# Stick-breaking heads: softplus of the last two key blocks added on the vector engine; blocks 0 and 1 multiply that sum instead of each block

## The chip, the cores and the metric

The kernel runs on one core of a Trainium2 chip. The metric is the time of one execution on the device in microseconds (us), as a median over runs; a profiled execution has its own time, which is given beside it. The core's engines are TensorE (PE in the profile, with its weight loads as PEld), VectorE (DVE), ScalarE (ACT), GpSimd (POOL) and SyncE (SP), which here only issues DMAs. Each engine takes its instructions in the order in which they were written into its own stream.

## The reference, cut to what matters

One transformer block over 512 tokens and 1024 channels: an adaptive modulation, sixteen stick-breaking attention heads of width 64, four retention heads, gates, a projection, and a feed-forward part. The change is in the stick-breaking heads, whose computation is this:

```python
def stick_breaking_attention(q, k, v):
    ...
    for i in range(s_len // BLOCK):
        end = (i + 1) * BLOCK
        ...
        z = jnp.einsum('bhtd,bhsd->bhts', qb, kb).astype(jnp.float32) * scale
        mask = s_pos[None, :] < t_pos[:, None]
        log_1m_beta = jnp.where(mask, jax.nn.log_sigmoid(-z), 0.0)
        after = lax.cumsum(log_1m_beta, axis=3, reverse=True) - log_1m_beta
        log_a = jax.nn.log_sigmoid(z) + after
        a = jnp.where(mask, jnp.exp(log_a), 0.0)
        outs.append(jnp.einsum('bhts,bhsd->bhtd', a.astype(v.dtype), vb))
```

For each query, log_sigmoid(-z) (which is minus the softplus of z) is summed over all later keys. A key block of 128 keys needs the sum inside the block and the full sums of every later block.

## The kernel before

**Tiling.** Activations lie with channels or keys on the 128 partitions and the 512 tokens along the row. Every product is made with operands split into a high and a low part (`split`, L205: ScalarE rounds a copy to the high part in L207, VectorE subtracts it for the low part in L209 or L210), so that one full product is three matmuls, and a product whose left side is exact (the triangle of minus ones `negtri`, the matrix of minus ones `negones`) is two. All matmuls are issued in the helper at L229.

**One head** (`sb_head`, L594). The scores stand with keys on the partitions and queries along the row. Key block j only meets queries from 128*j on, so the blocks are 512, 384, 256 and 256 columns wide. `GEO` (L111) gives each block its bank of the head's three `z` banks: block 0 is bank 0, block 1 is bank 1, and blocks 2 and 3 share bank 2, block 2 in columns 0 to 255 and block 3 in columns 256 to 511. The head then runs:
1. eight score matmuls, two for each block (L599), out of the tiles `q`;
2. softplus, bank by bank in the order 2, 1, 0: mask (VectorE, L607), minus the magnitude (VectorE, L609), Exp and Ln (ScalarE, L612 and L613), add the positive part (VectorE, L614), and a split into a tile `s` (L616);
3. the suffix sums, added on TensorE into the same `z` bank: for each block `negtri` times its own softplus and `negones` times that of every later block (L622 to L627), two matmuls for each term; then Exp (L630) and another split, which gives the attention weights of that bank;
4. eight matmuls with the values into one bank `av` (L639), a copy of it on ScalarE (L642), a DMA that moves half of it to the other partitions (L644, `t<-t`), and an add on VectorE (L645) that gives the head's output in `o`.

**What feeds a head.** `sb_qk` (L574) makes the queries and keys of a pair of heads: two products of 24 matmuls each into two `ps` banks, a split into two `qp` tiles (L561, L562), and eight DMAs (L567 to L570) that copy these into three `q` tiles, one for the keys of both heads and one for the queries of each.

**What runs between.** While a head waits for VectorE and ScalarE, TensorE works on products that depend on no head: `sb_qk` of later pairs and the branch gates (`mix`, 24 matmuls each into one `ps` bank). This text calls them filler. The loop at L1098 runs four groups of two pairs (four heads): it makes pairs 2g+2 and 2g+3 and some gates behind the heads of group g. Heads are numbered 0 to 15 and pairs 0 to 7 here. After the heads come the projections of `acts` (L1113 to L1131), which read all head outputs.

**What sets the order.** A scheduler sets the order on each engine in this part of the program when the kernel is built, by its own estimates of time and by free buffers; on the chip each engine then follows that order and waits at semaphores. The buffers that matter are in `BUFS` (L94): `q=8` tiles, `qp=2`, `ps=4` banks, `z=3` banks (one head's), `av=1`, `s=8`. A buffer is written again only when all readers of the tile before it are done. All loads go through the one queue of SP, in the order of its stream; a load that waits holds those behind it.

Of the kernel before, what the change touches and what calls it, by code (L numbers as in the profile page):

```python
# [19 lines left out]
P = 128  # L20
# [90 lines left out]
GEO = ((0, 0, 0, 512), (1, 0, 128, 384), (2, 0, 256, 256), (2, 256, 256, 256))  # L111
# [4 lines left out]
def kernel(  # L116
# [9 lines left out]
    nc = tc.nc  # L126
# [22 lines left out]
    def pair(tag):  # L149
        return apool.tile([P, 2, S], F32R, tag=tag, bufs=BUFS[tag], name=nm(tag))  # L150
# [44 lines left out]
    negtri = cpool.tile([P, P], F32R, name="negtri")  # L195
# [32 lines left out]
    def mm(o, lhs, rhs, start, stop):  # L228
        return nc.tensor.matmul(o, lhs, rhs, start=start, stop=stop, skip_group_check=True).ins  # L229
# [208 lines left out]
    with tc.manual_schedule(engines={nc.vector.engine, nc.scalar.engine, nc.tensor.engine}):  # L438

        nc.scalar.preload_act_table_set("natural_log_exp_and_others")  # L440
        c = sm[:, SM_C : SM_C + KT]
# [152 lines left out]
    def sb_head(h):  # L594
        q, k, vt = sbq[h], sbk[h], sbv[h // 4]
        z = [psz(), psz(), psz()]
        for j in (3, 2, 1, 0):
            bank, c, t0, w = GEO[j]
            for i in range(2):  # L599
                head_pe[h] = mm(z[bank][:, c : c + w], k[:, j * P : (j + 1) * P], q[:, i, t0:S],  # L600
                                i == 0 and j != 2, i == 1)
        sp = {}
        for bank in (2, 1, 0):
            w = BANKW[bank]
            zb = z[bank][:, :w]
            m = S if bank == 2 else P
            nc.vector.tensor_tensor(zb[:, :m], zb[:, :m], maskc[:, :m], op=ALU.min)  # L607
            t = tmp()[:, :w]
            nc.vector.tensor_scalar(  # L609
                t.bitcast(I32), zb.bitcast(I32), -(2**31), None, op0=ALU.bitwise_or  # L610
            )
            nc.scalar.activation(t, t, AF.Exp)  # L612
            nc.scalar.activation(t, t, AF.Ln, bias=1.0)  # L613
            nc.vector.scalar_tensor_tensor(t, zb, 0.0, t, op0=ALU.max, op1=ALU.add)  # L614
            hl = pair("s")
            split(hl[:, 0, :w], hl[:, 1, :w], t)  # L616
            sp[bank] = hl
        avs = {}
        for bank in (2, 1, 0):
            for j in (3, 2) if bank == 2 else (bank,):  # L620
                _, c, t0, w = GEO[j]
                terms = [(negtri, j, t0)] + [(negones, jj, GEO[jj][2]) for jj in range(j + 1, 4)]  # L622
                for lhs, jj, tt in terms:
                    bj, cj, tj, wj = GEO[jj]
                    for i in range(2):
                        mm(z[bank][:, c + tt - t0 : c + w], lhs, sp[bj][:, i, cj : cj + wj],
                           False, False)  # L627
            w = BANKW[bank]
            t = tmp()[:, :w]
            nc.scalar.activation(t, z[bank][:, :w], AF.Exp)  # L630
            hl = pair("s")
            split(hl[:, 0, :w], hl[:, 1, :w], t)
            avs[bank] = hl
        o = psa()
        r, hf = (h % 4) // 2, h % 2
        for j in (3, 2, 1, 0):
            bank, c, t0, w = GEO[j]
            v = vt[j // 2][:, j % 2, r * 256 + hf * P : r * 256 + hf * P + P]
            for i in range(2):  # L639
                mm(o[:, t0:S], v, avs[bank][:, i, c : c + w], j == 3 and i == 0, j == 0 and i == 1)  # L640
        u, u2 = tmp(), tmp()
        nc.scalar.activation(u, o, AF.Copy)  # L642
        own, oth = (slice(0, HD), slice(HD, P)) if hf == 0 else (slice(HD, P), slice(0, HD))
        nc.sync.dma_start(u2[own], u[oth])  # L644
        nc.vector.tensor_add(o_sb[h // 2][own], u[own], u2[own])  # L645
# [1082 lines left out]
```

## Time and profile before

| what | value |
|---|---|
| median of 3 runs | 1173.23 us (1172.66 to 1174.77) |
| profiled execution, its span | 1173.1 us |
| instructions on PE | 6476 matmuls, 1156.8 us busy (99% of the span) |
| DVE, ACT busy | 873.2 us (74%), 611.9 us (52%) |
| DMA | 192.88 MB, 164 GB/s mean |

The span runs from the first to the last instruction of the core. A group's row gives the number of instructions, the time in which any of them ran, and the mean length of one; matmuls are pipelined, so that the length of one (its latency) is longer than the distance at which the next one starts. In a timeline row the columns are start, length of the merged stretch, engine, line, operation, tiles, shapes and count. The heads lie between about 490 and 728 us.

### The profile page before, as it was taken

The page shows a single profiled execution, that of the slowest core. Times are in us where ns is not written, and L with a number is a line of the kernel's source. Part 1 is how long each engine was busy: PE and PEld are TensorE (multiplying, and loading weights), DVE is VectorE, ACT ScalarE, POOL GpSimd, SP SyncE. Part 2 cuts the span into 40 slices and gives each one's busy share as a digit, 9 for nine tenths or more (in the row PEclk, how much of TensorE's full clock was granted, in tenths as well). Part 3 has the DMA queues.
Part 4 walks back from the last instruction along what each step waited for, and adds up shares of the span by engine and source line. Part 5 has one row for each costly group of instructions (what it writes and reads, how often), then busy time and mean ns, then how long its engine had stood idle before and what let it go on. Part 6 is the DMA issues. An engine that isn't in the chain of part 4 may idle for free.

```text
span 1173.1 us, 16899 instructions
## 1 busy us (share of the span) xinstructions
PE 1156.8 (99%) x6476; PEld 1010.9 (86%) x6476; DVE 873.2 (74%) x1342; ACT 611.9 (52%) x928; POOL 50.1 (4%) x84
## 2 busy tenths in 40 slices
PE   8999999999999999999999999999999999999996
PEld 7898888888878888888888888879999999999996
DVE  7979966775764867478888688775998776777556
ACT  5444543343333444478778688354954444454433
POOL 0000000020002010000000000000100000000000
PEclk9999999999999999999999999999999999999999
DMA  9723536493566565846565545873545663565232
GB/s 358 256 68 113 185 103 208 154 260 115 161 201 176 181 159 185 232 123 180 153 173 133 153 126 179 283 235 103 113 136 179 184 161 116 148 186 152 86 89 72
DMA packets 64017, 192.88 MB, mean 164 GB/s; under 512 B 7744, under 2 KB 9920, under 8 KB 63936
## 3 DMA queue, kind: packets, MB, share of 16 engines
q1 hardware_dynamic: 56624, 172.92, 46.3%
q0 software_dynamic: 6768, 18.35, 8.8%
q8 instruction: 51, 0.84, 0.3%
q10 hardware_dynamic: 544, 0.52, 0.1%
q14 instruction: 30, 0.25, 0.1%
HBM read 146.15 MB, written 18.87 MB: 141 GB/s over the span
## 4 chain that ended last, share of the span: by engine, by line
PE 89%; DVE 4%; DMA 3%; ACT 2%; issue 1%; SPq 0%; DVEq 0%; ACTq 0%
PE ps L229 65%; PE z L229 21%; PE av L229 3%; DMA raw<-wp 2%; DMA araw<-wada 1%; DVE sraw L387 1%; ACT whi L207 1%; DVE wlo L209 1%; DMA o<-xT 0%; ACT s L207 0%; DVE wlo L418 0%; DVE t L425 0%; DVE araw L257 0%; DMA gspill<-g 0%; DVE t L476 0%
## 5 line engine op out<-in xcount | busy, mean ns | idle before, releaser
L229 PE MATMUL ps<-h,whi 128*128 128x512 f32 (+1 forms) x1410 | 416.9, 377 | 1.6 <-DVE h L209 0.8
L229 PEld LDWEIGHTS ps<-h,whi 128*128 128x128 f32 x1410 | 256.2, 188 | 47.7 <-ACT h L431 1.8
L229 PE MATMUL ps<-h,wlo 128*128 128x512 f32 (+1 forms) x705 | 262.1, 376 | 0.0
L207 ACT ACTIVATE whi<-raw 128x1024 fp32r<-128x1024 f32 (+1 forms) x122 | 127.4, 1044 | 192.3 <-PE ps L229 144.8
L209 DVE TENSOR_TENSOR wlo<-raw,whi 128x1024 fp32r<-128x1024 f32 (+1 forms) x122 | 146.6, 1204 | 61.9 <-ACT whi L207 60.8
L229 PEld LDWEIGHTS ps<-h,wlo 128*128 128x128 f32 x705 | 132.8, 188 | 23.2
L229 PE MATMUL ps<-s,whi 128*128 128x512 f32 x480 | 148.5, 390 | 0.7 <-DVE v L209 0.6
L229 PE MATMUL z<-q,whi 128*128 128x256 f32 x504 | 106.8, 283 | 0.0
L229 PEld LDWEIGHTS ps<-s,whi 128*128 128x128 f32 x480 | 89.2, 188 | 19.3 <-DVE v L209 1.0
L229 PE MATMUL ps<-s,wlo 128*128 128x512 f32 x240 | 93.4, 389 | 0.0
L207 ACT ACTIVATE s<-t 128x512 fp32r<-128x512 f32 (+1 forms) x134 | 74.4, 586 | 34.8 <-DVE t L789 21.4
L209 DVE TENSOR_TENSOR s<-t,s 128x512 fp32r<-128x512 f32 (+1 forms) x134 | 81.3, 637 | 9.6 <-ACT s L207 9.3
L229 PEld LDWEIGHTS z<-q,whi 128*128 128x128 f32 x504 | 84.9, 192 | 1.5
L1166 DVE SCALAR_TENSOR_TENSOR o<-ps,mod,o 128x512 f32<-128x512 f32 (+1 forms) x63 | 42.4, 680 | 32.6 <-PE ps L229 32.6
L229 PEld LDWEIGHTS ps<-s,wlo 128*128 128x128 f32 x240 | 45.1, 188 | 9.5
L877 ACT ACTIVATE whi<-s 128x1024 fp32r<-128x1024 f32 x33 | 34.9, 1056 | 33.6 <-PE ps L229 19.0
L229 PE MATMUL ps<-whi,h 128*128 128x512 f32 (+1 forms) x192 | 52.4, 354 | 0.0
L881 DVE TENSOR_TENSOR wlo<-s,whi 128x1024 fp32r<-128x1024 f32 x32 | 39.1, 1222 | 16.3 <-ACT whi L877 15.9
L229 PE MATMUL ps<-q,whi 128*128 128x256 f32 (+1 forms) x224 | 49.3, 313 | 0.0
L229 PE MATMUL z<-qp,whi 128*128 128x256 f32 x168 | 47.2, 283 | 0.0
L229 PE MATMUL z<-q,wlo 128*128 128x256 f32 x168 | 46.4, 283 | 0.0
L257 DVE SCALAR_TENSOR_TENSOR araw<-araw,cact 128x1024 f32<-128x1024 f32 x32 | 38.4, 1221 | 10.0 <-DMA araw<-wada 9.8
(311 smaller groups left out, 2063.1 us busy)
## 6 DMA issues: line engine op xcount, KB each, us to landing
raw<-wp SPq DMA_DIRECT2D x151, 512.0 KB, 4.0
araw<-wada SPq DMA_DIRECT2D x32, 512.0 KB, 4.5
araw<-wp SPq DMA_DIRECT2D x26, 512.0 KB, 4.6
sraw<-wada SPq DMA_DIRECT2D x16, 512.0 KB, 7.8
q<-qp SPq DMA_DIRECT2D x32, 256.0 KB, 3.7
s<-wp SPq DMA_DIRECT2D x12, 512.0 KB, 5.2
spill<-o POOLq DMA_DIRECT2D x24, 256.0 KB, 7.2
o<-xT SPq DMA_DIRECT2D x16, 256.0 KB, 3.7
```

The source lines that it names most:

```text
L207: nc.scalar.activation(dst_hi, src, AF.Copy, scale=scale)
L209: return (eng or nc.vector).tensor_sub(dst_lo, src, f(dst_hi))
L229: return nc.tensor.matmul(o, lhs, rhs, start=start, stop=stop, skip_group_check=True).ins
L257: nc.vector.scalar_tensor_tensor(raw, raw, 1.0, cact, op0=ALU.mult, op1=ALU.mult, accum_out=col)
L387: nc.vector.scalar_tensor_tensor(raw, raw, 1.0, cact, op0=ALU.mult, op1=ALU.mult, accum_out=col)
L877: nc.scalar.activation(hi, t, AF.Copy)
L881: nc.vector.tensor_sub(lo, t, f(hi))
L1166: return nc.vector.scalar_tensor_tensor(x1[d][:, hv], o[:, hv], mod[:, gcol + d : gcol + d + 1], x1[d][:, hv], op0=ALU.mult, op1=ALU.add,)
```

## The change

For each head, VectorE adds the softplus of block 3 to that of block 2 (256 columns, in place in the tile `t`), and the sum is split into a new tile `late` out of the `q` buffers. Blocks 1 and 0, which needed `negones` times block 2 and `negones` times block 3, now take `negones` times `late`. Block 2 still takes block 3 by itself, and block 0 still takes block 1. The suffix sums go from 20 matmuls a head to 16; the four that are gone are 256 columns wide.

```diff
--- before.py
+++ after.py
@@ -615,16 +615,24 @@
             hl = pair("s")
             split(hl[:, 0, :w], hl[:, 1, :w], t)
             sp[bank] = hl
+            if bank == 2:
+                late = pair("q")
+                nc.vector.tensor_add(t[:, 0:256], t[:, 0:256], t[:, 256:512])
+                split(late[:, 0, 0:256], late[:, 1, 0:256], t[:, 0:256])
         avs = {}
         for bank in (2, 1, 0):
             for j in (3, 2) if bank == 2 else (bank,):
                 _, c, t0, w = GEO[j]
-                terms = [(negtri, j, t0)] + [(negones, jj, GEO[jj][2]) for jj in range(j + 1, 4)]
-                for lhs, jj, tt in terms:
-                    bj, cj, tj, wj = GEO[jj]
+                terms = [(negtri, t0, sp[bank][:, :, c : c + w])]
+                if j == 2:
+                    terms.append((negones, 256, sp[2][:, :, 256:512]))
+                elif j < 2:
+                    if j == 0:
+                        terms.append((negones, P, sp[1][:, :, 0:384]))
+                    terms.append((negones, 256, late[:, :, 0:256]))
+                for lhs, tt, x in terms:
                     for i in range(2):
-                        mm(z[bank][:, c + tt - t0 : c + w], lhs, sp[bj][:, i, cj : cj + wj],
-                           False, False)
+                        mm(z[bank][:, c + tt - t0 : c + w], lhs, x[:, i, :], False, False)
             w = BANKW[bank]
             t = tmp()[:, :w]
             nc.scalar.activation(t, z[bank][:, :w], AF.Exp)
```

The scheduler works out a new order for everything from the first head on. In what follows names carry the number that the build gave them, and lines behind the diff are 8 higher in the changed kernel.

**SP's queue, the loads of the queries and keys of pair 4 (heads 8 and 9).** `q_1007` and `q_1015` are the keys, `q_1008`, `q_1009`, `q_1016` and `q_1017` the queries of the two heads; `t<-t` is the half of a head's output that changes partitions, `t_941` of head 4, `t_1004` of head 7. Before:

```order
L567 DMA q_1008_5266<-qp_1005_5259 64x1024
L568 DMA q_1008_5266<-qp_1005_5259 64x1024
L644 DMA t_941_4931<-t_940_4930 64x512
L202 DMA raw_1114_5819<-wp 128x1024
L569 DMA q_1007_5265<-qp_1006_5260 64x512
L567 DMA q_1009_5271<-qp_1005_5259 64x1024
L570 DMA q_1007_5265<-qp_1006_5260 64x512
L568 DMA q_1009_5271<-qp_1005_5259 64x1024
L569 DMA q_1007_5265<-qp_1006_5260 64x512
L570 DMA q_1007_5265<-qp_1006_5260 64x512
```

With the change:

```order
L202 DMA raw_1158_6024<-wp 128x1024
L567 DMA q_1016_5266<-qp_1013_5259 64x1024
L568 DMA q_1016_5266<-qp_1013_5259 64x1024
L569 DMA q_1015_5265<-qp_1014_5260 64x512
L570 DMA q_1015_5265<-qp_1014_5260 64x512
L567 DMA q_1017_5271<-qp_1013_5259 64x1024
L652 DMA t_1004_5193<-t_1003_5192 64x512
L568 DMA q_1017_5271<-qp_1013_5259 64x1024
L569 DMA q_1015_5265<-qp_1014_5260 64x512
L570 DMA q_1015_5265<-qp_1014_5260 64x512
```

The eight loads stood around the output copy of head 4; they now stand behind six more weight loads, and the last three of them behind the output copy of head 7.

**TensorE, the scores of head 8 and the first suffix sum of its bank 2.** `z_1038`, `z_1037`, `z_1036` before and `z_1046`, `z_1045`, `z_1044` now are banks 2, 1 and 0 of head 8; `ps` rows are filler; `av_994` and `av_1002` are head 7's. Before (the rows left out are filler):

```order
L229 MATMUL z_1037_5439<-q_1008_5266,q_1007_5265 128x384 x2
L229 MATMUL z_1036_5438<-q_1008_5266,q_1007_5265 128x512 x2
L229 MATMUL ps_1109_5787<-h_57_256,whi_1112_5791 128x512
L229 MATMUL ps_1109_5787<-h_57_256,wlo_1113_5792 128x512
L229 MATMUL av_994_5183<-s_993_5180,v_745_3838 128x512
L229 MATMUL ps_1109_5787<-h_68_303,whi_1112_5791 128x512 x2
...
L229 MATMUL ps_1110_5788<-h_57_256,whi_1115_5821 128x512 x2
L229 MATMUL z_1038_5440<-s_1040_5455,negtri_96 128x256
```

With the change:

```order
L229 MATMUL ps_1122_5788<-h_118_532,whi_1127_5821 128x512
L229 MATMUL ps_1122_5788<-h_118_532,wlo_1128_5822 128x512
L229 MATMUL av_1002_5183<-s_1001_5180,v_745_3838 128x512
L229 MATMUL z_1046_5440<-q_1016_5266,q_1015_5265 128x256 x4
L229 MATMUL z_1045_5439<-q_1016_5266,q_1015_5265 128x384 x2
L229 MATMUL z_1044_5438<-q_1016_5266,q_1015_5265 128x512 x2
L229 MATMUL ps_1134_5866<-h_40_217,whi_1136_5869 128x512
L229 MATMUL z_1046_5440<-s_1048_5455,negtri_96 128x256
L229 MATMUL ps_1134_5866<-h_40_217,whi_1136_5869 128x512
L229 MATMUL z_1046_5440<-s_1048_5455,negtri_96 128x256 x3
```

Before, 25 matmuls of filler and two of `av` stand between the last scores of head 8 and its first `negtri`; now one matmul of filler stands there, and its bank `ps_1134` is the one that `ps_1023`, the queries of pair 5, has held.

**TensorE, the suffix sums of head 15, the last one.** `z_1215`, `z_1214`, `z_1213` before and `z_1230`, `z_1229`, `z_1228` now are its banks 2, 1 and 0; `q_1233` is its `late`; `ps_1256` and `ps_1272` are the last gate. Before:

```order
L229 MATMUL ps_1256_6636<-h_90_398,wlo_1259_6640 128x512
L229 MATMUL z_1215_6366<-s_1217_6381,negtri_96 128x256
L229 MATMUL ps_1256_6636<-h_101_445,whi_1258_6639 128x512 x2
L229 MATMUL z_1214_6365<-s_1219_6390,negtri_96 128x384
L229 MATMUL z_1215_6366<-s_1217_6381,negtri_96 128x256 x3
L229 MATMUL z_1215_6366<-s_1217_6381,negones_97 128x256 x2
L229 MATMUL z_1214_6365<-s_1219_6390,negtri_96 128x384
L229 MATMUL z_1214_6365<-s_1217_6381,negones_97 128x256 x4
L229 MATMUL z_1213_6364<-s_1221_6399,negtri_96 128x512 x2
L229 MATMUL z_1213_6364<-s_1219_6390,negones_97 128x384 x2
L229 MATMUL z_1213_6364<-s_1217_6381,negones_97 128x256 x4
```

With the change:

```order
L229 MATMUL ps_1272_6636<-h_118_532,wlo_1275_6640 128x512
L229 MATMUL z_1230_6366<-s_1232_6381,negtri_96 128x256
L229 MATMUL z_1229_6365<-s_1235_6394,negtri_96 128x384
L229 MATMUL z_1230_6366<-s_1232_6381,negtri_96 128x256 x3
L229 MATMUL z_1230_6366<-s_1232_6381,negones_97 128x256 x2
L229 MATMUL z_1229_6365<-s_1235_6394,negtri_96 128x384
L229 MATMUL z_1228_6364<-s_1237_6403,negtri_96 128x512 x2
L229 MATMUL z_1228_6364<-s_1235_6394,negones_97 128x384 x2
L229 MATMUL z_1229_6365<-q_1233_6384,negones_97 128x256
L229 MATMUL z_1228_6364<-q_1233_6384,negones_97 128x256
L229 MATMUL z_1229_6365<-q_1233_6384,negones_97 128x256
L229 MATMUL z_1228_6364<-q_1233_6384,negones_97 128x256
```

Before, the last gate's filler went on between and behind the suffix sums of head 15; now its last matmul stands ahead of them.

## The prediction

> **What bounds the kernel now.** I read the clock of the core first, then the page's chain of waits, then the stretch in which the heads run, by windows.
>
> ```profile
> core 0: 1173.1 us, clock 0.998
> PE 89%; DVE 4%; DMA 3%; ACT 2%; issue 1%; SPq 0%; DVEq 0%; ACTq 0%
> PE ps L229 65%; PE z L229 21%; PE av L229 3%; DMA raw<-wp 2%; DMA araw<-wada 1%; DVE sraw L387 1%; ACT whi L207 1%; DVE wlo L209 1%; DMA o<-xT 0%; ACT s L207 0%; DVE wlo L418 0%; DVE t L425 0%; DVE araw L257 0%; DMA gspill<-g 0%; DVE t L476 0%
> 490.00:740.00 250.00, 249.95 (x1268) 209.31 (x1267) 201.93 (x335) 194.52 (x351) 0.00 (x0) 1.00 0.56 160
> ```
>
> The chain that ends last is 89% TensorE. In the window 490 to 740 us, all of the heads, TensorE runs for 249.95 of 250 us at full clock, VectorE for 201.93 (81%) and ScalarE for 194.52 (78%). So what leaves TensorE here leaves the time, as long as the next matmul in its order is always ready. That is a condition: two engines at about 80% are close behind, and a head is a chain through them.
>
> **The saving.** The removed matmuls, in the groups of that window and in the timeline of TensorE:
>
> ```profile
> L229 PE MATMUL z<-s,negones 128*128 128x256 f32 x160 | 26.8, 281 | 0.0
> 708.48 0.63 PE L229 MATMUL z<-s,negones 128*128 128x256 f32 x4
> 708.95 0.39 PE L229 MATMUL ps<-h,whi 128*128 128x512 f32 x1
> ```
>
> One is 281 ns long, but that is latency: four of them start at 708.48 and the next matmul at 708.95, so each occupies 0.47 / 4 = 0.1175 us. Four a head over 16 heads are 64, and 64 x 0.1175 = **7.5 us** off TensorE. By this scale 512 columns are 0.23 us, and I count TensorE's work in the orders with it.
>
> **The added work.** Each head gets one add and one subtraction on VectorE and one copy on ScalarE, of 256 columns. The nearest rows:
>
> ```profile
> L209 DVE TENSOR_TENSOR s<-t,s 128x256 fp32r<-128x256 f32 x8 | 2.9, 418 | 0.0
> L207 ACT ACTIVATE s<-t 128x256 fp32r<-128x256 f32 x8 | 2.8, 404 | 0.4 <-DVE t L1040 0.4
> ```
>
> That is 0.84 us on VectorE and 0.40 on ScalarE a head, 13.4 and 6.5 us in all. VectorE goes from 81% to about 86% of the stretch. It lies beside filler, so I cost it at nothing wherever filler stands behind the head's own matmuls; with no filler at all it would be up to 1.24 us a head, 20 us. Where filler is missing it is paid, and the orders show two such places. Everywhere else the work that stands between the last scores of a head and its first `negtri` is 5.2 us or more after the change; before it was as low as 4.5 us (heads 4 and 12), with TensorE at 249.95 of 250.
>
> **Stall one, head 8.** `late` takes one of the eight `q` tiles in every head, so the tiles of pair 4 come free later and its loads are issued later (the order of SP). The last three now stand behind the output copy of head 7. Until all are read, the two `qp` tiles stay full; pair 5 (`ps_1023`, `ps_1024`) can't be split into them, pair 6 (`ps_1121`, `ps_1122`) stands behind it, and these four are all four `ps` banks. Filler has no bank. The rows for the walk, from ScalarE, VectorE and SP around the last head before, and from the groups and DMA views:
>
> ```profile
> 714.66 0.60 ACT L642 ACTIVATE t<-av 128x512 f32<-128x512 f32 x1 [1.31 <-PE av L229]
> 715.15 1.04 ACT L612 ACTIVATE t<-t 128x512 f32<-128x512 f32 x2
> 719.77 1.55 ACT L207 ACTIVATE s<-t 128x512 fp32r<-128x512 f32 x3
> 721.75 1.05 ACT L207 ACTIVATE whi<-raw 128x1024 fp32r<-128x1024 f32 x1
> 722.70 0.95 ACT L630 ACTIVATE t<-z 128x512 f32<-128x512 f32 x2
> 715.28 0.47 SPq L644 DMA_DIRECT2D t<-t  x1
> q<-qp SPq DMA_DIRECT2D x32, 256.0 KB, 3.7
> L207 ACT ACTIVATE qp<-ps 128x512 fp32r<-128x512 f32 x12 | 7.0, 582 | 0.5 <-PE ps L229 0.5
> L210 DVE SCALAR_TENSOR_TENSOR qp<-ps,qp 128x512 fp32r<-128x512 f32 x6 | 4.1, 682 | 0.0
> ```
>
> Let T be the end of head 7's last `av` matmul. ScalarE first makes a weight's high part, which had to wait for the filler that ends just ahead of T (0.95 us from one start to the next, 721.75 to 722.70), then the output copy: T + 1.55. SP issues its DMA (0.47 us) and then the next query load at T + 2.1, which lands 3.7 us later, T + 5.8. ScalarE and VectorE split `ps_1023` (0.58 and 0.68 us): the first filler matmul can start at T + 7.1. TensorE has only the eight scores of head 8 in that time, 2816 columns or 1.3 us. **Idle 5.8 us.** The first `negtri` needs an Exp and a copy more on ScalarE (0.52 us each in the rows of two and three) and comes at T + 7.45; from there head 8's softplus and the two splits of pair 5 take turns on both engines with one or two filler matmuls between, and walking them in their order I find waits of 0.1, 0.35, 0.2, 0.5, 0.35 and 0.1 us: 1.6 more. Together **7.4 us**. From below: if the loads came at no cost, the chain from mask to copy is still six operations (0.7 and 0.7 on VectorE, 0.6 and 0.6 on ScalarE, 0.7 and 0.6), 3.9 us, less 0.2 of filler, 3.7. From above, full lengths in place of distances between starts: 8.2.
>
> **Stall two, head 15.** The order shows the last gate's filler ending ahead of the first `negtri` of head 15. After that only the first products of the projections are left, and their operands (`acts`) are queued behind head 15 on ScalarE and VectorE.
>
> ```profile
> 712.59 0.98 PE L229 MATMUL z<-q,q 128*128 128x384 f32 x4
> 717.40 0.75 DVE L827 TENSOR_SCALAR g<-ps,sm 128x512 f32<-128x512 f32 x1 [1.47 <-PE ps L229]
> 718.07 0.68 DVE L645 TENSOR_TENSOR o<-t,t 64x512 f32<-64x512 f32 x1
> 718.67 1.74 DVE L614 SCALAR_TENSOR_TENSOR t<-z,t 128x512 f32<-128x512 f32 x3
> 720.42 1.76 DVE L209 TENSOR_TENSOR s<-t,s 128x512 fp32r<-128x512 f32 x3
> 720.61 0.28 PE L229 MATMUL z<-s,negtri 128*128 128x256 f32 x1
> 722.83 1.23 DVE L209 TENSOR_TENSOR wlo<-raw,whi 128x1024 fp32r<-128x1024 f32 x1 [0.65 <-ACT whi L207]
> t<-t SPq DMA_DIRECT2D x16, 128.0 KB, 2.2
> ```
>
> Before, head 15's last scores end at about 713.5 (the row at 712.59) and its first `negtri` is at 720.61: 7 us, filled. Now 3.8 us of work stands there. Let U be the end of head 14's last `av` matmul: the filler ends at U + 2.3. VectorE's order still has head 14's output add (L645) ahead of head 15's L614. The output copy is done at U + 0.9, its DMA lands 2.2 us later, the add ends at U + 3.8, L614 at U + 4.5, ScalarE's copy at U + 5.2: **2.9 us idle**. Then the remaining steps come at the pace of VectorE's three subtractions (1.76 us); I find 0.33, 0.45 and 0.4 us for banks 1, 2 and 0. `late` comes last of all: a weight's high part (0.95 us) and low part (1.23 us) stand ahead of its copy and its subtraction, so its low half waits 0.85 us. The `av` matmuls and the first products of the projections then wait about 0.7 us in all. Together **5.6 us**; from below 2.9 (only the first wait), from above 6.9 (full lengths).
>
> **The clock after stall one.** The trace has one long stretch without matmuls, its end:
>
> ```profile
> 1163.42 0.59 PE L229 MATMUL z<-t,ones 128*128 128x256 f32 x2
> 1165.00:1167.00 2.00, 0.00 (x0) 0.00 (x0) 1.89 (x5) 0.00 (x0) 0.00 (x0) 1.00 0.50 164
> 1167.00:1169.00 2.00, 0.00 (x0) 0.00 (x0) 2.00 (x5) 0.00 (x0) 0.00 (x0) 0.56 0.48 159
> ```
>
> The last matmul ends at 1164.01. The granted clock is 1.00 up to 1167 and 0.56 in the mean over the next 2 us, so it falls to one half at about 1167.24, 3.2 us after the last matmul. A gap of 5.8 us is longer than that. What then runs at half clock is head 8's first suffix sums, filler and head 9's first scores, 2.2 us by count, which double; some of it fills waits I have already counted. I take **1.5 us**, between 0 (no fall) and 5 (all of head 8's 4.9 us of work up to its last `av`). How soon the clock comes back no row here shows. The Trainium skill, "TensorE: Matmul & The Clock Gate", section "Part 1: The HAM clock gate (the "warmup" mystery)", says the clock halves after about 3.4 us of idleness and returns after about 3.4 us of sustained work, in windows that run freely. The trace agrees on the fall (3.2 us). By that page's figures the estimate is 3.4 us at half speed, so a cost up to 1.7 us if TensorE were fully busy.
>
> **The sum.** 1173.1 - 7.5 + 7.4 + 5.6 + 1.5 = 1180.1 us for a profiled execution. Its own time, 1173.1, agrees with the median of 1173.23, so nothing is added. The forecast is **1180.1 us**.
>
> **The rivals.**
> 1. *The saving lands whole.* SP and the two engines keep ahead, the stalls vanish, 1173.1 - 7.5 = 1165.6 us. For it: TensorE is never idle now and VectorE has 19% free. Against it: after the eight scores of head 8 TensorE's order holds one matmul of filler, and it can't pass a waiting one. It decides if pair 4's loads reach the `qp` release before T, which the output copy of head 7 excludes. 10%.
> 2. *Short stalls.* Both at their lower bounds, no fall of the clock: 1173.1 - 7.5 + 3.7 + 2.9 = 1172.2 us. For it: idle time lets the other engines run ahead, and a load can land sooner than its median. 16%.
> 3. *Both stalls, clock stays.* 1178.6 us. For it: a fall after 3.2 us is seen once, at the end. This is the same forecast without its last term. 20%.
> 4. *The loop of each head gets longer.* `late` ends about 3 us behind a head's first `negtri`, and the orders put its low half 2.9 to 3.9 us behind it, just in time. If half of the added 0.84 us on VectorE shows in every head, 16 x 0.4 = 6.4 us come on top: 1186.5 us. Against it: the other just-in-time steps before left TensorE 0.05 us idle in 250. 10%.
>
> **How the numbers follow.** My forecast has 42%, which leaves 2% for what I have not thought of. Forecast and rival 3, one mechanism with and without its last term, hold 62% and lie at 1178 to 1182 us. For 8 in 10 the range leaves out rival 1 and most of rival 4: 1171.5 to 1186 us. Of the chances, taking 0.2% (2.3 us) as what a measurement here can tell from no change: faster needs less than 1170.9, rival 1 and the fast edge of rival 2, 11%; no difference is most of rival 2, 14%; slower is the rest, 75%.
>
> **What would show it.** Right: 128 `negones` matmuls in place of 192, 0.1175 us apart; TensorE idle for 5 to 7 us in one piece after head 7's last `av`, ended by VectorE's subtraction into `qp`; about 3 us idle ahead of head 15's first `negtri`, ended by ScalarE's copy into `s`; the granted clock below 1.00 in a window just behind the first gap and nowhere else. The time up to head 0's suffix sums and from the projections on should not move by itself. Wrong: TensorE still at 249 of 250 us (rival 1), one of the two gaps absent, or an idle time of about 0.4 us in every head (rival 4).

## The result, and the profile after

The changed kernel takes 1177.6 us (median of 7 runs, 1176.8 to 1179.3) where the kernel before takes 1174.5 us in the same comparison (7 runs, 1172.7 to 1175.1). The ratio is 1.0028, with a 95% interval from 1.0018 to 1.0039: slower by 3.1 us, and by more than the 0.2% that can be told from no change. The profiled execution spans 1175.9 us against 1173.1.

First the same lines as before the change: the clock and span of the core, the chain of waits by engine, and the window of all heads (busy time of TensorE, its weight loads, VectorE, ScalarE and GpSimd, then the granted clock, the DMA share and GB/s).

```profile
core 0: 1175.9 us, clock 0.990
PE 93%; DVE 3%; ACT 2%; DMA 1%; issue 1%; SPq 0%; DVEq 0%; ACTq 0%
490.00:740.00 250.00, 241.81 (x1181) 200.91 (x1180) 208.38 (x358) 198.60 (x365) 0.00 (x0) 0.97 0.52 149
```

TensorE was busy for 249.95 of these 250 us and is now for 241.81, and the clock has come down to 0.97. The waits of TensorE from 600 to 735 us, in us in total, times, and the longest, name two places:

```profile
PE ps L229 <- DVE qp L210: 4.7, 1, 4.7
PE z L229 <- ACT s L207: 3.0, 2, 2.7
PE z L229 <- DMA q<-qp: 0.5, 1, 0.5
```

The first place in the timeline (start, length, engine, line, operation; in brackets the idle time before and what ended it; SPq is SyncE's DMA queue):

```profile
609.47 0.41 PE L229 MATMUL av<-s,v 128*128 128x512 f32 x1
610.40 0.58 ACT L650 ACTIVATE t<-av 128x512 f32<-128x512 f32 x1
610.42 1.53 PE L229 MATMUL z<-q,q 128*128 128x256 f32 x8 [0.54 <-DMA q<-qp]
611.01 0.46 SPq L652 DMA_DIRECT2D t<-t  x1
611.52 0.59 SPq L568 DMA_DIRECT2D q<-qp  x1
615.06 0.57 ACT L207 ACTIVATE qp<-ps 128x512 fp32r<-128x512 f32 x1
...
615.90 0.68 DVE L210 SCALAR_TENSOR_TENSOR qp<-ps,qp 128x512 fp32r<-128x512 f32 x1
616.64 0.80 PE L229 MATMUL ps<-h,whi 128*128 128x512 f32 x1 [4.69 <-DVE qp L210]
```

This is head 8. Head 7's last `av` matmul starts at 609.47, its output copy at 610.40, the copy's DMA at 611.01, and only behind that the next load of pair 4 (`q<-qp`, 611.52). When the loads have read `qp`, ScalarE and VectorE split the waiting bank into it, and filler (`ps<-h,whi`) starts at 616.64. The second place is head 15:

```profile
720.83 0.39 PE L229 MATMUL ps<-h,wlo 128*128 128x512 f32 x1
721.93 0.67 DVE L653 TENSOR_TENSOR o<-t,t 64x512 f32<-64x512 f32 x1
722.52 1.74 DVE L614 SCALAR_TENSOR_TENSOR t<-z,t 128x512 f32<-128x512 f32 x3
723.23 1.69 ACT L207 ACTIVATE s<-t 128x512 fp32r<-128x512 f32 x3
723.92 1.58 PE L229 MATMUL z<-s,negtri 128*128 128x256 f32 x3 [2.70 <-ACT s L207]
```

The last filler matmul starts at 720.83. VectorE then has head 14's output add ahead of head 15's `L614`, ScalarE copies behind that, and the first `negtri` starts at 723.92. Windows around the two places show what the clock did (its granted share is the third number from the right):

```profile
612.00:617.00 5.00, 0.36 (x1) 0.36 (x2) 4.90 (x11) 3.82 (x8) 0.00 (x0) 0.70 0.96 234
617.00:621.00 4.00, 4.00 (x16) 3.50 (x16) 3.30 (x8) 2.91 (x7) 0.00 (x0) 0.52 1.01 298
621.00:625.00 4.00, 4.00 (x24) 3.37 (x23) 1.58 (x4) 0.81 (x3) 0.00 (x0) 1.00 0.98 224
...
724.00:728.00 4.00, 4.00 (x13) 3.38 (x14) 3.83 (x7) 3.98 (x8) 0.00 (x0) 0.50 0.00 0
728.00:732.00 4.00, 4.00 (x19) 3.63 (x18) 3.03 (x6) 3.90 (x9) 0.00 (x0) 0.74 0.79 215
```

TensorE counts as busy in 617 to 621 and 724 to 728, but at half clock: 16 and 13 matmuls in 4 us where the window at full clock, with another mix of widths, has 24.

To compare whole stretches, I take from the traces the **lost time** of TensorE: from the start of each matmul to the start of the next, less the pace at full clock (0.227, 0.177 and 0.118 us for 512, 384 and 256 columns, the medians of the trace before). It holds idle time and half clock alike. In us:

| stretch | before | after | difference |
|---|---|---|---|
| 490 to 605, heads 0 to 7 | 4.3 | 3.2 | -1.0 |
| 605 to 625, head 8 | 0.6 | 8.0 | +7.5 |
| 625 to 718 | 2.5 | 2.6 | +0.1 |
| 718 to 740, head 15 | 0.1 | 6.1 | +6.0 |
| 740 to 790, projections | 1.7 | 0.6 | -1.1 |
| sum | 9.1 | 20.5 | +11.4 |

The 64 removed matmuls are 64 x 0.118 = 7.6 us. So 11.4 - 7.6 = 3.8 us are left; with 0.8 us less lost time ahead of 490 us that is 3.0, and the spans differ by 2.8. The change saved what it was to save and lost it again in two places.

### The profile page after: what moved, and what is told of

It is laid out like the page before. It is cut to its first block, busy times and chain, and to the rows that moved or that the text cites. A ratio compares the mean times of both kernels' runs of the same rounds, so it can differ in the third digit from the quotient of the medians.

```text
span 1175.9 us, 16809 instructions
## 1 busy us (share of the span) xinstructions
PE 1153.7 (98%) x6412; PEld 1007.5 (86%) x6412; DVE 884.5 (75%) x1374; ACT 618.3 (53%) x944; POOL 50.1 (4%) x84
## 4 chain that ended last, share of the span: by engine, by line
PE 93%; DVE 3%; ACT 2%; DMA 1%; issue 1%; SPq 0%; DVEq 0%; ACTq 0%
PE ps L229 69%; PE z L229 22%; PE av L229 3%; ACT whi L207 1%; DVE wlo L209 1%; DMA q<-qp 0%; DMA araw<-wada 0%; DVE araw L257 0%; DVE t L476 0%; DMA o<-xT 0%; DMA t<-t 0%; DVE o L653 0%; DVE t L614 0%; ACT s L207 0%; DVE fin L1619 0%
## 5 line engine op out<-in xcount | busy, mean ns | idle before, releaser
L229 PE MATMUL z<-q,q 128*128 128x256 f32 (+2 forms) x224 | 45.7, 331 | 0.5 <-DMA q<-qp 0.5
```

## The experiments

Two theories were to be told apart. **Mine:** the two places have causes of their own, above all the `q` buffer that `late` takes, and the added work elsewhere is hidden. **The rival:** the added work on VectorE and ScalarE lengthens every head, and the places only show where that comes due. All times are medians, and the ratio is to the kernel before, run in the same comparison (1174.1, 1174.2 and 1173.9 us in the three comparisons). Every edit also makes a new order of everything from the first head on, so what an edit is worth includes what its order is worth; where only gates move and no stall is there, that was 1.0 us (e8) and 0.5 us (e11).

### 1 and 2: one stall taken away at a time

Run e1 gives `late` a buffer of another class:

```diff
-                late = pair("q")
+                late = pair("s")
```

> One edit to the changed kernel: late takes an s buffer (of eight) in place of a q buffer; the sum, its split and the matmuls stay. Theory (the q buffer delays pair 4's loads, and that empties TensorE at head 8): the order now has 7.0 us of work between head 8's scores and its first negtri, where the changed kernel has 0.2, and 4.8 us at head 15, where it has 3.8. The idle 4.9 us at head 8 and the half clock behind it go: about 7.3 us less (8.3 us lost there, less 1.0 that such a stretch loses anyway), and about 1 us less idle at head 15: 1177.6 - 8.3 = 1169.3 us, between 1167 and 1171.5; TensorE never idle for over 1 us between 600 and 640. Rival (the added work on VectorE and ScalarE costs the time, in whatever buffer it lands): 1176.5 to 1178.5 us. If the s buffers are as scarce as the q buffers: a new gap of several us at another head, 1174 or more.

Run e2 moves one gate from the second group to the last:

```diff
-    for g, n in enumerate((2, 2, 4, 6)):
+    for g, n in enumerate((2, 1, 4, 7)):
```

> One edit to the changed kernel: of the gates, one fewer is laid behind the second group of heads and one more behind the last (2, 1, 4, 7 for 2, 2, 4, 6); late stays in a q buffer. Theory (stall two is a lack of filler at head 15): the order has 7.2 us ahead of head 15's first negtri where the changed kernel has 3.8, and still 0.2 us at head 8. Stall two and the half clock behind it go, 6.4 - 0.9 = 5.5 us; stall one stays as it is (4 to 5 us idle and half clock). 1177.6 - 5.5 = 1172.1 us, between 1170.5 and 1174.5, the upper end because head 7 has only 3.6 us of work now. Rival (head 15 is held by its own chain with late, whatever is laid ahead): no gain, 1176.5 to 1178.5 us.

Measured: e1 1177.62 us, ratio 1.0028 [1.0017, 1.0040], the time of the changed kernel; e2 1181.74 us, 1.0065 [1.0051, 1.0079]. Both forecasts failed. The windows of head 8 and head 15 in e1:

```profile
605.00:625.00 20.00, 20.00 (x102) 16.28 (x101) 17.63 (x31) 14.17 (x28) 0.00 (x0) 1.00 0.78 222
...
718.00:740.00 22.00, 19.24 (x78) 15.19 (x77) 13.23 (x24) 12.62 (x25) 0.00 (x0) 0.84 0.48 146
```

The mechanism was right and its worth was not. The gap at head 8 is gone (20.00 of 20 us busy, clock 1.00), but head 15 now loses 6.7 us, and the projections behind it 4.2 (2.5 of them two waits for the low parts of weights on VectorE). In e2 the gap at head 15 went as expected (2.4 us lost from 718 to 740), and others opened, one of them in the projections (4.0 us, with half clock from 777.70 to 781.11). Its windows ahead of head 8 and at it:

```profile
600.00:603.60 3.60, 1.99 (x10) 1.25 (x9) 2.87 (x5) 3.60 (x7) 0.00 (x0) 1.00 0.88 183
603.60:610.40 6.80, 6.61 (x22) 4.85 (x20) 4.72 (x9) 4.39 (x9) 0.00 (x0) 0.50 0.31 77
610.40:617.20 6.80, 2.10 (x11) 1.44 (x10) 5.14 (x11) 4.25 (x9) 0.00 (x0) 1.00 0.62 133
```

Head 7, with one gate less, waits 1.6 us in all in the first row, and that is followed by 6.8 us at half clock; head 8's gap stays (third row). A stall taken away in one place came up in another. The theory that the two places are the causes, each by itself, fell here.

### 3 and 4: each half of the change alone

Run e3 adds `late`, split from block 3 alone, and removes nothing. Run e4 removes the matmuls and adds nothing; its blocks 0 and 1 leave out the softplus of block 2, so it serves for the time alone:

```diff
 e3, against the changed kernel
-                split(late[:, 0, 0:256], late[:, 1, 0:256], t[:, 0:256])
+                split(late[:, 0, 0:256], late[:, 1, 0:256], t[:, 256:512])
...
+                    terms.append((negones, 256, sp[2][:, :, 0:256]))
                     terms.append((negones, 256, late[:, :, 0:256]))
 e4, against the changed kernel
-            if bank == 2:
-                late = pair("q")
-                nc.vector.tensor_add(t[:, 0:256], t[:, 0:256], t[:, 256:512])
-                split(late[:, 0, 0:256], late[:, 1, 0:256], t[:, 0:256])
...
-                    terms.append((negones, 256, late[:, :, 0:256]))
+                    terms.append((negones, 256, sp[2][:, :, 256:512]))
```

> All that the change adds and nothing that it removes: late is added, copied and subtracted in a q buffer as in the changed kernel, but split from block 3 alone, and blocks 0 and 1 multiply block 2 and late each (192 negones matmuls, as before the change). The order has 7.5 us ahead of head 8's first negtri, 7.0 at head 15 and no head below 4.5. Theory (the added work is hidden wherever filler stands behind the scores; the time is lost in the two holes of the order): the time of the kernel before, 1174.5, within 1.5 us. Rival (VectorE and ScalarE are too close behind, each head pays 0.3 to 0.5 us): 1174.5 + 5 to 8 = 1179 to 1182 us, with idle times of 0.3 us or more in most heads. If the q buffer alone makes the late loads stall TensorE: a gap of several us at head 8, 1177 or more.

> All that the change removes and nothing that it adds: late is not computed, and blocks 0 and 1 multiply block 3's softplus alone and leave out block 2's (64 matmuls of 256 columns less). The order has no head below 4.5 us of work ahead of its first negtri. Theory (the removed matmuls are worth 0.1175 us each as long as filler stands in the order): 1174.5 - 7.5 = 1167.0 us, between 1165.5 and 1168.5, no gap over 1 us between 490 and 740. Rival (the heads are chains through VectorE and ScalarE, and what leaves TensorE comes back as waiting): 1171 to 1174.5 us, with many small idle times.

Measured: e3 1176.98 us, 1.0022 [1.0013, 1.0031], so +2.8; e4 1167.79 us, 0.9945 [0.9932, 0.9958], so -6.4. The saving is real. The span of e4's trace is 7.0 us shorter than before (1166.1), though it has 1.4 us more lost time, 10.5 against 9.1, all of it between 740 and 790 us (3.3 against 1.7). The added work alone costs 2.8 us, between the two theories' figures. The two halves would add up to about -3.5, and both together make +3.1: 6.6 us more. Something runs short only when both are there. Head 8 shows it: in e3, too, `late` takes a `q` buffer, and the last load of pair 4 is issued at 601.51 us, 28 us later than before (573.57), yet only 0.5 us are lost from 605 to 625. With the matmuls gone as well it is issued at 612.79, and head 8 stalls. At head 15 e3 loses 2.3 us, where the kernel before loses 0.1 and the changed kernel 6.1.

### 5, 6 and 10: the place of the added work

All three start from e1 (`late` in an `s` buffer). Run e5 makes late's sum and low part on GpSimd, e6 writes its three operations behind bank 0's softplus instead of behind bank 2's, e10 behind bank 1's:

```diff
 e5
-                nc.vector.tensor_add(t[:, 0:256], t[:, 0:256], t[:, 256:512])
-                split(late[:, 0, 0:256], late[:, 1, 0:256], t[:, 0:256])
+                nc.gpsimd.tensor_add(t[:, 0:256], t[:, 0:256], t[:, 256:512])
+                split(late[:, 0, 0:256], late[:, 1, 0:256], t[:, 0:256], eng=nc.gpsimd)
 e6 (e10: bank == 1 in place of bank == 0)
             if bank == 2:
+                t2 = t
+            if bank == 0:
                 late = pair("s")
-                nc.vector.tensor_add(t[:, 0:256], t[:, 0:256], t[:, 256:512])
-                split(late[:, 0, 0:256], late[:, 1, 0:256], t[:, 0:256])
+                nc.vector.tensor_add(t2[:, 0:256], t2[:, 0:256], t2[:, 256:512])
+                split(late[:, 0, 0:256], late[:, 1, 0:256], t2[:, 0:256])
```

> The version with late in an s buffer (1177.62 us, no gap at head 8, the loss now at head 15), and in it the addition and the subtraction that make late run on GpSimd instead of VectorE; the copy stays on ScalarE. Theory (filler budget: the added 0.84 us of VectorE a head, 13.4 us in all, lengthens each head's chain, TensorE covers it with filler from the heads behind, and the filler is used up before head 15): without it on VectorE the heads need no more cover than in the kernel without late, so 1168 to 1171 us, and TensorE is idle less than 1.5 us in all around head 15. If only the missing 7.5 us of TensorE work makes the filler short, VectorE's share is not the price: 1176 to 1178.5 us. If GpSimd is slow (no row of the trace shows an addition there), block 1 waits for late in each head: 0.3 us or more a head, 1180 or more.

> The version with late in an s buffer, and in it the three operations that make late written behind bank 0's softplus instead of behind bank 2's: same work, same buffers, only behind the work of banks 1 and 0 on VectorE and ScalarE. The order has 5.2 us or more ahead of every head's first negtri, 7.0 at head 15. Theory (late stands in the chain of banks 1 and 0 and delays them): the chain is shorter by up to 0.84 us a head, 1168 to 1173 us. If it is VectorE's total work and not its place: 1176 to 1178.5 us. If late now comes too late for block 1's sum: a wait for it in most heads, 1180 or more.

> Late in an s buffer, made behind bank 1's softplus: between the version that makes it behind bank 2's (1177.62 us) and the one behind bank 0's (1166.43 us). The order has 5.9 us or more ahead of every first negtri and 7.2 at head 15. Theory (what late delays is the chain of the banks behind it): only bank 0's is delayed, so in between, 1168 to 1174 us. Rival (it is one accident of the order at head 15, where the first version has 4.8 us ahead and this has 7.2): 1166 to 1168 us, as with late last.

Measured: e5 1178.01 us, 1.0035 [1.0022, 1.0048]; e6 **1166.43 us, 0.9936 [0.9924, 0.9948]**; e10 1171.38 us, 0.9973 [0.9962, 0.9983]. The same three operations behind bank 2, bank 1 and bank 0 take 1177.6, 1171.4 and 1166.4 us: the work is as large in each, and the edit moves only its place (the scheduler then orders the rest anew). The middle one is not clean: e10 loses 6.7 us more than e6, and 3.5 of them lie between 490 and 605 us, around one wait of 2.1 us and a half-clock stretch from 563.62 to 567.03. ScalarE in one head of e1, and in one of e6:

```profile
650.67 0.61 ACT L207 ACTIVATE s<-t 128x512 fp32r<-128x512 f32 x1
651.37 1.06 ACT L207 ACTIVATE whi<-raw 128x1024 fp32r<-128x1024 f32 x1
652.79 0.63 ACT L836 ACTIVATE g<-g 128x512 f32<-128x512 f32 x1 [0.36 <-DVE g L835]
653.33 1.33 ACT L207 ACTIVATE s<-t 128x256 fp32r<-128x256 f32 x3
```

```profile
658.70 1.55 ACT L207 ACTIVATE s<-t 128x512 fp32r<-128x512 f32 x3
660.15 0.62 ACT L839 ACTIVATE g<-g 128x512 f32<-128x512 f32 x1
660.67 1.05 ACT L207 ACTIVATE whi<-raw 128x1024 fp32r<-128x1024 f32 x1
661.63 0.40 ACT L207 ACTIVATE s<-t 128x256 fp32r<-128x256 f32 x1
```

In e6 the copies of banks 2, 1 and 0 follow one another (x3), and late's copy, 256 wide, comes 2.9 us later. In e1 late's copy is first of the second group of three: it has to wait for VectorE's sum, a weight and a gate are put into that wait, and banks 1 and 0 stand behind all of it, some 3 us behind bank 2, where e6 has about 0.5 us from one to the next. TensorE is not idle meanwhile; it runs filler. How much, the rows of the output copy tell, that of head 0 and that of head 14, in e1 and in e6:

```profile
507.77 0.60 ACT L650 ACTIVATE t<-av 128x512 f32<-128x512 f32 x1 [1.71 <-PE av L229]
720.60 0.60 ACT L650 ACTIVATE t<-av 128x512 f32<-128x512 f32 x1 [1.35 <-PE av L229]
```

```profile
507.79 0.60 ACT L652 ACTIVATE t<-av 128x512 f32<-128x512 f32 x1 [1.34 <-PE av L229]
711.38 0.60 ACT L652 ACTIVATE t<-av 128x512 f32<-128x512 f32 x1 [0.66 <-PE av L229]
```

14 heads take 212.8 us in e1 and 203.6 in e6, 15.2 and 14.5 us each. Counted by the pace above, TensorE runs 68.6 us of the heads' own matmuls in both, but 136.2 us of filler (gates, pairs and 4.5 us of projections) in e1 against 129.6 in e6, and loses 8.0 against 5.3. So the filler of e1 is spent 6.6 us sooner. Its last filler matmul before a gap starts at 724.03 us, just ahead of head 15's first `negtri` (724.26), and the next one at 733.79; in e6 filler goes on until 722.36, 1.4 us ahead of head 15's last `av`.

Run e5 came out in the range of its rival, but it tells little on that, because its price is another one: over the same 14 heads it has 127.8 us of filler, less than e6, but 16.3 us of lost time. GpSimd's two operations and one of VectorE's, as groups of the heads' window (count, busy us, mean ns):

```profile
L209 POOL TENSOR_TENSOR s<-t,s 128x256 fp32r<-128x256 f32 x16 | 16.5, 1032 | 10.0 <-ACT s L207 10.0
L620 POOL TENSOR_TENSOR t<-t 128x256 f32<-128x256 f32 x16 | 13.1, 821 | 266.2 <-DVE s L209 266.2
```

```profile
L209 DVE TENSOR_TENSOR s<-t,s 128x384 fp32r<-128x384 f32 x32 | 23.9, 747 | 8.2 <-ACT s L207 8.0
```

The addition takes 0.82 us and the subtraction 1.03 where VectorE needs 0.42 for either, and VectorE's own subtractions of 384 columns, 553 ns in e1, now take 747 in the mean (those of 512 columns take 684 in both). Lost time is spread over the heads (6.5, 5.0 and 5.5 us up to 605, 625 and 718). The Trainium skill, "Trainium Architecture — The Big Picture", section "What this means for kernel authors", says that VectorE and GpSimd share one pair of memory ports under an exclusive lock; the 194 ns more are what that would look like, though the runs do not show a lock as such.

### 7 and 8: more filler

Run e7 is e1 with one of the two early gates laid under the heads; e8 is the control, the same edit on the kernel before:

```diff
-            mix(1)
-    for g, n in enumerate((2, 2, 4, 6)):
+            mix(1 - p)
+    for g, n in enumerate((2, 3, 4, 6)):
```

> The version with late in an s buffer, and one gate (24 matmuls of 512 columns, 5.7 us of TensorE by the order) laid under the heads instead of ahead of them: one early gate instead of two, and 2, 3, 4, 6 behind the groups. Nothing is computed more or less. Theory (filler budget: the heads lack cover at their end): the loss around head 15 falls by up to 5.7 us, 1172 us, between 1170.5 and 1174.5. Rival (the loss is head 15's own chain, for which no gate is left to wait): 1176.5 to 1178.5 us. Rival (the gate is missed as filler ahead of the heads): a new idle time before 498 us, and no gain.

> The control for the gate: the kernel before the change, with the same gate moved under the heads. In the kernel before, filler ends 0.5 us ahead of the last av matmul of head 15, so it lacks none, and TensorE is never idle there. Theory (filler budget): no gain, 1174.1 us within 1.5. Rival (a gate under the heads is worth something in itself, whatever the change): 1169 to 1172 us, as in the kernel with late.

Measured: e7 1170.50 us, 0.9969 [0.9958, 0.9980], 7.1 us below e1; e8 1173.15 us, 0.9992 [0.9983, 1.0001], no change that can be told. A gate's 24 matmuls more under the heads bring 7 us where `late` stands first, and nothing in the kernel before. That is what a shortage of filler looks like: the kernel before had just enough (its last filler starts 0.5 us ahead of head 15's last `av`), and with `late` behind bank 2 (e1) more was used than there was.

### 9: the buffer again, with late in its good place

Run e9 is e6 with the `q` buffer of the changed kernel:

```diff
-                late = pair("s")
+                late = pair("q")
```

> The fastest version so far (late in an s buffer, made behind bank 0's softplus, 1166.43 us) with one edit: late takes a q buffer again. The order has 0.0 us of work between head 8's scores and its first negtri, and 4.5 at head 15. Theory (the q buffer delays pair 4's loads, and with no filler behind it that costs 5 us of idle time at head 8 and half clock behind it, wherever late is made): 1166.4 + 7.3 = 1173.7 us, between 1171 and 1176; one gap of 4 to 6 us after head 7, ended by the split into qp. Rival (the place of late in the chain is all that counts, the buffer nothing): 1166 to 1168 us.

Measured: 1182.45 us, 1.0061 [1.0047, 1.0075], 16.0 us above e6. The buffer alone, which was worth nothing in e1, is worth 16 us here, over twice the 7.3 of my theory. Its windows of head 8 and head 15:

```profile
605.00:625.00 20.00, 15.20 (x67) 12.45 (x67) 14.27 (x25) 11.89 (x24) 0.00 (x0) 0.83 0.66 167
...
718.00:740.00 22.00, 17.96 (x73) 14.09 (x73) 16.52 (x29) 18.79 (x35) 0.00 (x0) 0.84 0.54 178
```

Both places are back, 7.9 and 8.2 us lost. For head 8, the last load of pair 4 in e6, and the output copy's DMA with the loads of pair 4 behind it in e9:

```profile
562.82 0.62 SPq L570 DMA_DIRECT2D q<-qp  x1
```

```profile
612.08 0.46 SPq L654 DMA_DIRECT2D t<-t  x1
612.59 0.59 SPq L568 DMA_DIRECT2D q<-qp  x1
613.23 0.59 SPq L569 DMA_DIRECT2D q<-qp  x1
613.86 0.62 SPq L570 DMA_DIRECT2D q<-qp  x1
```

The same load is issued 51 us later. For head 15, the low parts of the projections' operands, which take `q` buffers too (`acts`, the first four), in the changed kernel and in e6:

```profile
728.86 0.69 DVE L209 TENSOR_TENSOR q<-o,q 128x512 fp32r<-128x512 f32 x1
731.39 1.89 DVE L209 TENSOR_TENSOR q<-o,q 128x512 fp32r<-128x512 f32 x3
```

```profile
653.22 1.28 DVE L209 TENSOR_TENSOR q<-o,q 128x512 fp32r<-128x512 f32 x2
669.20 0.69 DVE L209 TENSOR_TENSOR q<-o,q 128x512 fp32r<-128x512 f32 x1
684.30 0.68 DVE L209 TENSOR_TENSOR q<-o,q 128x512 fp32r<-128x512 f32 x1
```

With `late` in `s` buffers they are ready some 20 us before head 15's scores (706.3 in e6), and the first products of the projections serve as its filler: 6.4 us of them run ahead of its last `av` in e6, and 1.6 in the changed kernel. In e9 these low parts start at 732.99 us and later, and 1.8 us of the projections run ahead. So the second stall has the buffer for a cause as well.

### 11 and 12: two checks on the fast version

Run e11 is e6 with one early gate under the heads (2, 2, 4, 7). Run e12 is e3 with `late` as in e6, behind bank 0's softplus and in an `s` buffer.

```diff
 e11, against e6
-            mix(1)
-    for g, n in enumerate((2, 2, 4, 6)):
+            mix(1 - p)
+    for g, n in enumerate((2, 2, 4, 7)):
 e12, against e3
             if bank == 2:
-                late = pair("q")
+                t2 = t
+            if bank == 0:
+                late = pair("s")
...
-                split(late[:, 0, 0:256], late[:, 1, 0:256], t[:, 256:512])
+                split(late[:, 0, 0:256], late[:, 1, 0:256], t2[:, 256:512])
```

> The fastest version so far, and one early gate laid under the heads in addition (one early gate, and 2, 2, 4, 7 behind the groups). Theory (with late last the heads do not run short of filler; TensorE's only waits left there are 1.84 and 0.44 us in the projections): little to gain, 1164.5 to 1167 us. If filler were still short: 5.7 us less, 1161 us. It also tells whether 1166.4 hangs on one order of the gates.

> All that the change adds and nothing that it removes, as in the third experiment (1176.98 us, 2.8 over the kernel before), but with late in an s buffer and made behind bank 0's softplus; late is split from block 3 alone, and blocks 0 and 1 multiply block 2 and late each (192 negones matmuls). Theory (the price of the added work is its place in the chain): the kernel before's time, 1174.2 us within 1.2. Rival (the price is the 13.4 us of VectorE, wherever they stand): 1176 to 1178 us.

Measured: e11 1166.88 us, 0.9935 [0.9922, 0.9947]; e12 1173.49 us, 0.9995 [0.9986, 1.0003]. With `late` last the heads no longer lack filler, so a gate more brings nothing, and the 1166.4 us do not hang on one order of the gates. And all 20 us of added work on VectorE and ScalarE cost nothing in the good place and buffer, where e3 paid 2.8 us. The two differ in place and buffer at once, and their filler over the 14 heads is alike (125.8 and 125.5 us), so they do not tell which of the two e3 paid for.

Put together, one edit apart in each row and column:

| late made behind | in a `q` buffer | in an `s` buffer |
|---|---|---|
| bank 2 (the change: `q`) | 1177.6 | 1177.6 |
| bank 1 | not run | 1171.4 |
| bank 0 | 1182.5 | 1166.4 |

Either fault by itself is enough to lose the saving, so mending one alone brought nothing. e6 is faster than both kernels.

## Why the prediction was right, and where it was not

**The time.** 1180.1 us was forecast, 1177.6 was measured, inside the range and on the side that was given 75%. By its terms, against the lost times of the first section:

- *The saving, -7.5.* Right: 64 x 0.118 us, and alone (e4) it shows as -7.0 in the span and -6.4 in the medians.
- *Stall one, +7.4, and the clock behind it, +1.5.* 8.9 forecast, 7.5 measured, and at the place, with the releaser and by the walk that was given. The first filler started 6.8 us after the end of head 7's last `av` (609.88), and T + 7.1 was forecast. The idle piece is 4.7 us in the row (4.9 as lost time) and not 5.8, because the scores of head 8 began 0.5 us late and ran to 611.95; that is just short of the 5 to 7 us that were named as the sign. The small waits, that 0.5 us included, are 1.1 us and not 1.6; half clock costs 2.1 us (4.2 us of work at half pace) and not 1.5.
- *Stall two, +5.6.* 6.0 measured, with 2.7 us idle in the row (2.9 as lost time, as forecast) ahead of the first `negtri`, ended by ScalarE's copy into `s`. The rest came about otherwise: the further waits are 0.7 us and not 2.7, and some 2.4 us are half clock, which the prediction excluded ("nowhere else"). That the sum still fits within 0.4 us is luck.
- *What was missing in the sum.* Waits that the kernel before had became shorter: 1.1 us around 775 us, 1.0 in heads 0 to 7, 0.8 ahead of 490. The forecast held these stretches to be unmoved; 2.9 us too high there is most of the miss of the span (1180.1 against 1175.9).

**The step that does not hold** is "it lies beside filler, so I cost it at nothing wherever filler stands behind the head's own matmuls". The added work was indeed hidden head by head, and rival 4's idle time in every head did not appear. But filler that hides something is spent, and there is a fixed amount of it. e1 against e6 shows 6.6 us of it spent by head 14 for nothing but the place of three operations; e7 and e8 show that a gate more is worth 7 us with `late` in that place and nothing in the kernel before. The forecast came out all the same because in the changed kernel the buffer costs the time first: its filler over the 14 heads is 129.8 us, as in e6, and e9, with the good place, has both stalls too. The price of the place shows once the buffer is mended. Rival 4 was right that a head can get longer, 15.2 us in e1 against 14.5 in e6, and wrong about where this is paid: at the end, for lack of filler, and not as idle time in every head.

**Stall one's cause** was given as the `q` buffer, and e1 and e9 show it: with `s` the last load of pair 4 is issued at 562.8 us (e6), with `q` at 613.9 (e9), and with `s` the gap at head 8 is gone. The buffer does this together with the saving: in e3, without the saving, its loads came late and head 8 did not wait. What does not follow, and what I took to follow in the expectations of e1 and e2, is that the time comes back when the gap goes. For **stall two** the prediction had the right effect (the operands of the projections come too late to serve as filler) with half its cause: not only are they queued behind head 15, they have no `q` buffer before.

**The rivals.** The saving that lands whole (1165.6 us) needed pair 4's loads early; with that and late last it is e6, 1166.4. Short stalls: the measured ones are not short, though the profiled sum lies between that case and the forecast. Both stalls with the clock staying at full (1178.6 us): this time is nearer to the measured one than the forecast's, by luck, for the clock fell behind both.

**The clock rule.** The prediction weighed the Trainium skill, "TensorE: Matmul & The Clock Gate", section "Part 1: The HAM clock gate (the "warmup" mystery)", where idleness of about 3.4 us halves the clock, beside a fall 3.2 us after the last matmul at the end of the trace before. Here it fell 2.1 and 2.0 us after the end of the last matmul (611.95 to 614.03, 721.22 to 723.26), and stayed at half for 6.8 us, while that section of the Trainium skill has about 3.4 us of sustained work until it returns. The fall came sooner than after 3.4 us of idleness. The return does not contradict the section, because TensorE was busy for only 0.80 and 2.75 us in the first 3.41 us at half clock, and where it was busy for all of them (617.27 to 620.68 in e2, 563.62 to 567.03 in e10) the clock was back after 3.41 us.

**Left open.** Why e9 is 4.8 us slower than the changed kernel, both in `q`, stays open; of its additional lost time 2.1 us lie at head 15 and 1.7 between 625 and 718 us. A buffer of late's own, apart from `q` and `s`, was not tried. What the clock costs by itself, with a stall kept and TensorE held busy through it, was not tried either.

## What to carry to other kernels

Where one engine is kept full by filler, price an addition not by whether something hides it but by how much filler hides it, and look at the end of the filler, not at the place of the addition. A new tile in a shared class of buffers is a change to every load and copy that takes the next buffers of that class, here the loads of the next pair and operands that another stage could have had over 40 us sooner. And when the removal of a stall brings nothing, don't drop its cause: two causes can each suffice, and only the table of both edits shows it.

## What the hardware showed that I had not expected

The half-clock stretches have edges on a common grid. In the changed kernel they run from 16.70 to 20.11, 614.03 to 620.86 and 723.26 to 730.08 us: 3.41 us once and 6.83 twice, and the starts lie 175 and 207 steps of 3.413 us apart from the first. So the clock seems to be set per window of 3.41 us by what TensorE did in the window before. Four such windows, the last before a fall in e10, in e5 and in e2, and one in e4 behind which the clock stayed:

```profile
560.21:563.62 3.41, 1.30 (x9) 1.15 (x9) 3.09 (x6) 1.77 (x3) 0.00 (x0) 1.00 1.08 205
```

```profile
618.01:621.42 3.41, 1.56 (x9) 1.35 (x10) 3.38 (x7) 2.10 (x3) 0.53 (x1) 1.00 0.65 147
```

```profile
600.21:603.62 3.41, 1.80 (x9) 1.10 (x8) 2.89 (x5) 3.41 (x7) 0.00 (x0) 1.00 0.89 183
```

```profile
765.04:768.45 3.41, 1.73 (x8) 1.11 (x6) 1.80 (x4) 1.47 (x2) 0.00 (x0) 1.00 0.78 275
```

TensorE was busy for 1.30, 1.56 and 1.80 us ahead of the falls, and for 1.73 us where none followed, so its busy time does not separate them. Busy time holds the latency of the last matmul before each gap. Counted at the pace of the lost time instead, the four windows hold 1.07, 1.42 and 1.27 us of work ahead of the falls and 1.56 where none followed. That would fit a limit somewhere between 1.42 and 1.56 us, but four windows do not show one. A gap of about 2 us was enough for a fall in e10 (one wait of 2.1 us), and its phase against the grid seems to decide. A window spent at half clock does half the work, so it can cost up to 1.7 us. Two stretches do not fit: ahead of the falls at 16.70 us in the changed kernel and at 17.26 in e5 TensorE was busy for 3.28 of 3.41 us, and the kernel before shows no fall there. They are left open.
